# A transformer trunk on one core: two block pairs of the FFN's first product per layer as seven block products instead of eight

## The chip, the cores and the metric

The kernel runs on one core of one Trainium2 chip. The metric is the device time of one execution in microseconds (us); less is better.

## What is computed

Two layers of an encoder block over 256 tokens of width 1024, all in float32. The part that matters here, cut from the reference:

```python
h = h + rms_norm(mixed @ w_out, g_mix_post)                       # "wout"

gate, up = jnp.split(rms_norm(h, g_ffn_pre) @ w_ffn_in, 2, axis=-1)   # "ffnin": 1024 x 5632
h = h + rms_norm((jax.nn.silu(gate) * up) @ w_ffn_out, g_ffn_post)    # "ffnout": 2816 x 1024

e = p_i @ w_ple_proj                                              # "emb": 256 x 1024
h = h + rms_norm(jax.nn.sigmoid(h @ w_ple_gate) * e, g_ple_post)      # "ple"
```

Ahead of it in each layer stand one wide projection, gated linear attention and grouped-query attention, which the change does not touch.

## The kernel before

**Three matmuls for one product.** Each operand is kept as a high part rounded to the chip's float32r and a low part, the rest. `split` (L99) makes both: ScalarE copies (a CAST in the profile, L101), VectorE subtracts (L97). `mm3` (L87) then adds high x high, high x low and low x high into one PSUM bank. So a product of 128 tokens x 512 rows of weights x 512 columns is 4 x 3 = 12 matmuls of 128x512.

**The weight stream.** `plan` is the list of all weight units in the order of their use; a unit is 128 x 2048 (1 MB; 512 rows x 512 columns). `Stream` loads units on the SP queue into two `raw` buffers, splits each in two halves of 1024 into one of four pairs of buffers `wh` and `wl`, hands them out with `take` and gets them back with `done`. `ws = Stream(4)`: at most four units are split and not yet given back. `done` calls `fill`, which splits the next unit and starts the load behind it, so a split begins when TensorE has finished with the unit four before.

**ffnin.** The hidden width of 2816 is cut into 11 blocks of 256 (`NBLK`). A unit of a block holds 256 gate columns and 256 up columns for one half of the 1024 rows (`unit_gate_up`, L136), so a block is two units, and a unit is 24 matmuls: two token halves `hf` of 128 by 12. Blocks 0 and 1 go token half by token half with all four units held; blocks 2 to 10 go through `project` unit by unit. Then ScalarE takes silu of the gate half out of PSUM and VectorE multiplies by the up half ("gating"); some matmuls later TensorE transposes the result and `split` puts it into `hid`, the left operand of ffnout.

**Order of work around it.** The program is traced in one order, and a scheduler at compile time orders each engine's queue by it and by the times that it assumes. `tick()`, after every two rows of a unit's matmuls, counts down `Task`s, which put small work (transposes, attention steps) between the matmuls. `by_half` (L430) runs wout and ple with the first token half complete before the second, so that the norm of one half lies beside the matmuls of the other. Behind wout come the 24 matmuls of ple_proj (part "emb", L1015), and then ffnin (L1027), which needs the second half's norm after its first 36 matmuls. ffnout (L1075) and ple (L1109) follow. The input p is transposed ahead of wout.

**Buffers.** `big`: nine of 128 x 2048; `mid`: ten of 128 x 1024; `t512`: five; PSUM: eight banks (`acc`, `aux`).

Of the kernel before, what the change touches and what calls it, by code (L numbers as in the profile page):

```python
# [2 lines left out]

# [27 lines left out]
HIDDEN = 2816  # L31
NBLK = HIDDEN // 256
UNIT = 2112
RQ = ((0, 288), (288, 672), (672, 1056))
# [5 lines left out]
def trunk_kernel(ctx: ExitStack, tc: tile.TileContext, a: dict, out: bass.AP):  # L40
# [122 lines left out]
    for l in range(DEPTH):  # L163
        w = a["w_in"][l]
        plan += [unit_rows(w, n, C_RA, C_RA + 1056, 2 if l + n == 0 else 1) for n in range(4)]
        for c0 in (C_AK, C_GQ, C_GK, C_GV, C_GV + 512, C_GG, C_GG + 512, C_GA, C_GA + 512, C_GB, C_GB + 512):
            plan += [unit(w, kh, c0) for kh in range(2)]
        for j in range(2):
            for wo in (a["w_o_gla"][l], a["w_o_attn"][l]):
                plan += [unit(wo, kh, j * 512) for kh in range(2)]  # L170
        plan += [unit(a["w_out"][l], kh, j * 512) for kh in range(2) for j in range(2)]
        plan += [unit_rows(a["w_ple_proj"][l], 0)]
        plan += [unit_gate_up(a["w_ffn_in"][l], kh, b) for b in range(NBLK) for kh in range(2)]
        plan += [unit_rows(a["w_ffn_out"][l], n) for n in range(NBLK)]
        plan += [unit(a["w_ple_gate"][l], kh, j * 512) for kh in range(2) for j in range(2)]

    class Stream:


        def __init__(self, depth):  # L180
            self.depth, self.n, self.held, self.raws, self.ready, self.open = depth, 0, 0, [], [], False

        def load(self, between=lambda: None):

            if self.n == len(plan):
                return
            raw = rawp.tile([P, UNIT], F32, tag="raw", name=nm("raw"))
            moves = plan[self.n](raw)
            for dst, src in moves:
                if self.open:  # L190
                    nc.sync.dma_start(dst, src)
                else:
                    on("dma", nc.sync.dma_start, dst, src)
                between()
            self.raws.append((raw, sum(math.prod(dst.shape[1:]) for dst, _ in moves)))
            self.n += 1

        def pieces(self):

            raw, n = self.raws.pop(0)  # L200
# [4 lines left out]
            return [(wh[:, c], wl[:, c], raw[:, c]) for c in (slice(0, n // 2), slice(n // 2, n))]  # L205

        def fill(self):
            while self.open and self.held < self.depth and self.raws:
                for piece in self.pieces():
                    split(*piece)  # L210
                self.load()

# [4 lines left out]
        def done(self, n=1):  # L217
            self.held -= n
            self.fill()

# [37 lines left out]
    class Split:  # L258


        def __init__(self):
            self.h, self.l = (big(F32R).rearrange("p (k t) -> p k t", t=T) for _ in range(2))
            self.makers = {0: [], 1: []}

        def need(self, hf, k=None):
# [9 lines left out]
        def put(self, src, k, n, t0, tn):  # L275

            i = (slice(None), slice(k, k + n), slice(t0, t0 + tn))
            split(self.h[i], self.l[i], src.rearrange("p (k t) -> p k t", t=tn))

        def tok(self, k, hf):  # L280
            s = slice(hf * P, (hf + 1) * P)
            return self.h[:, k, s], self.l[:, k, s]

        def all(self, k):
            return self.h[:, k, :], self.l[:, k, :]

    def transpose_in(sp, src, k, n, hf):

        ps = aux()
        for i in range(n):  # L290
            nc.tensor.transpose(ps[:, i * P : (i + 1) * P], src[:, i * P : (i + 1) * P], ident)
        with tc.high_priority(AHEAD):
            sp.put(ps[:, : n * P], k, n, hf * P, P)

    last_pow = [None]
# [47 lines left out]

    def turn_in(sp, x, hf, wait):


        def turn():
            yield wait
            for j, y in enumerate(halves(x)):
                transpose_in(sp, y, 4 * j, 4, hf)  # L350

        sp.makers[hf].append(Task(turn(), part[0]))

    def pre_norm(g, hf, sp, wait=WAIT):

# [6 lines left out]

        turn_in(sp, xn, hf, wait)

# [27 lines left out]
    def wmode(os_, sp, k0, w, first, last):  # L392
# [9 lines left out]
        for f in range(4):  # L402
            o = os_[f // 2][:, (f % 2) * T : (f % 2 + 1) * T]
            s = slice(f * P, (f + 1) * P)
            for k in range(4):
# [3 lines left out]
                )  # L409
            tick()  # L410

    def project_t(sp):
# [113 lines left out]
    def turned(hf, k, n):  # L526

        ps = aux()
        for i in range(n):
            on("pe", nc.tensor.transpose, ps[:, i * P : (i + 1) * P], xn[hf][:, (k + i) * P : (k + i + 1) * P], ident)  # L530
        i = (slice(None), slice(k, k + n), slice(hf * P, (hf + 1) * P))
        split_here(uT.h[i], uT.l[i], ps[:, : n * P].rearrange("p (k t) -> p k t", t=P))

# [42 lines left out]
    for l in range(DEPTH):  # L576
# [413 lines left out]

        part[0] = f"{l}emb"
        e = big().rearrange("p (s c) -> p s c", s=2)
        pin = t512().rearrange("p (s c) -> p s c", c=256)
        nc.sync.dma_start(pin, a["p"][l, 0].rearrange("(s p) c -> p s c", p=P))
        pT = [t.rearrange("p (k t) -> p k t", t=T) for t in halves(mid(F32R))]
        ps = aux()
        for k in range(2):
            for hf in range(2):
                nc.tensor.transpose(
                    ps[:, k * T + hf * P : k * T + (hf + 1) * P], pin[:, hf, k * P : (k + 1) * P], ident  # L1000
                )
        split(pT[0], pT[1], ps.rearrange("p (k t) -> p k t", t=T))
# [4 lines left out]
        u2 = Split()  # L1007

        def after_out(hf, o):
            post_norm_add(o, gpost, hf)  # L1010
            pre_norm(gpre, hf, u2)

        by_half(mixT, after_out)

        part[0] = f"{l}emb"  # L1015
        wh, wl = (t[:, :2048].rearrange("p (k c) -> p k c", c=512) for t in ws.take())
        for hf in range(2):
            s = slice(hf * P, (hf + 1) * P)
            for j in range(2):
                o = acc()  # L1020
                for k in range(2):
                    mm3(o, (pT[0][:, k, s], pT[1][:, k, s]), (wh[:, 2 * k + j, :], wl[:, 2 * k + j, :]), k == 0, k == 1)
                nc.scalar.copy(e[:, hf, j * 512 : (j + 1) * 512], o)
        ws.done()


        part[0] = f"{l}ffnin"  # L1027
        hid = [Split() for _ in range(3)]
        us = [[ws.take() for _ in range(2)] for _ in range(2)]
        for hf in range(2):  # L1030
            for b in range(2):
                o = acc()
# [5 lines left out]
                nc.scalar.activation(sg[:, 0:256], o[:, 0:256], AF.Silu)  # L1038
                vmul(sg[:, 0:256], o[:, 256:512], sg[:, 0:256])


                def turn(sg=sg, b=b, hf=hf):
                    yield WAIT_FFN
                    transpose_in(hid[0], sg[:, 0:256], b * 2, 2, hf)

                hid[0].makers[hf].append(Task(turn(), part[0]))
        for b in range(2, NBLK):
            sg = t512()
            for hf, o in enumerate(project(u2)):
                c = slice(hf * 256, (hf + 1) * 256)  # L1050
                nc.scalar.activation(sg[:, c], o[:, 0:256], AF.Silu)
                vmul(sg[:, c], o[:, 256:512], sg[:, c])

            def turn(sg=sg, b=b):
                yield WAIT_FFN
                ps = aux()
                for k in range(2):
                    for hf in range(2):
                        nc.tensor.transpose(
                            ps[:, k * T + hf * P : k * T + (hf + 1) * P],  # L1060
                            sg[:, hf * 256 + k * P : hf * 256 + (k + 1) * P], ident,
                        )
                with tc.high_priority(AHEAD):
                    hid[b // 4].put(ps, 2 * b % 8, 2, 0, T)

            turned = Task(turn(), part[0], 2 * b % 8 // 4)
            for hf in range(2):
                hid[b // 4].makers[hf].append(turned)

        if l + 1 < DEPTH:  # L1070
            ropes = rope_tables(l + 1)
            wup_next = up_weights(l + 1)


# [5 lines left out]
        def out_step(n, hf, w):  # L1080
            wh, wl = (t[:, :2048].rearrange("p (k c) -> p k c", c=512) for t in w)
            for kk in range(2):
                k = 2 * n + kk
                hid[k // 8].need(hf, k % 8)
                for j in range(2):
                    mm3(
                        o[hf][j], hid[k // 8].tok(k % 8, hf), (wh[:, 2 * kk + j, :], wl[:, 2 * kk + j, :]),
                        k == 0, k == 2 * NBLK - 1,
# [10 lines left out]
        for hf in range(2):  # L1099
# [5 lines left out]

            turn_in(hT, h[:, hf, :], hf, WAIT_H)


# [77 lines left out]
```

## Time and profile before

| | |
|---|---|
| Time, median of 3 runs | 950.26 us (949.28 to 950.45) |
| The profiled execution | 950.44 us, span 948.7 us |
| TensorE clock granted | 0.998 of full speed |
| TensorE (PE) busy | 936.2 us, 99% of the span |
| VectorE (DVE) busy | 612.8 us, 65% |
| ScalarE (ACT) busy | 509.9 us, 54% |
| DMA | 169.25 MB, mean 178 GB/s |

In the profile a line starts with the line number in the kernel; names of buffers carry the layer and the part (`acc_0ffnin` is a PSUM bank of ffnin in layer 0). A group's row gives its count, its busy time and the mean duration in ns of one instruction; behind the last bar stands how long the engine was idle just before these, and what ended that. The chain of waits follows the work that ended last back from the end, and shows on which engine the time of the whole program lay.

### The profile page before, as it was taken

Reading aid. Unit: us, or ns where it says so; the run is one execution under the profiler, and the core shown is the slowest. Engines: PE = TensorE matmul, PEld = TensorE weight load, DVE = VectorE, ACT = ScalarE, POOL = GpSimd, SP = SyncE. Lnnn points to the kernel's source line nnn. Section 1 sums busy time; section 2 is a strip of 40 time slices with the busy share of each in tenths; the row PEclk is TensorE's granted clock in tenths of the full one; section 3 lists DMA queues with packets and bytes.
Section 4 is the critical chain, followed back from the end, with each engine's and each line's share of the span. In section 5 each row is a group of like instructions: output and inputs, shape, how many; then the busy total and the mean of one; then the engine's idle time right before and its main releaser. Section 6 shows DMA issues by size and latency. Waiting matters only on the chain.

```text
span 948.7 us, 12370 instructions
## 1 busy us (share of the span) xinstructions
PE 936.2 (99%) x4769; PEld 798.5 (84%) x4769; DVE 612.8 (65%) x838; ACT 509.9 (54%) x872; POOL 83.3 (9%) x152
## 2 busy tenths in 40 slices
PE   8999999999999999999999999999999999999996
PEld 7998888888888888888889988888888888888886
DVE  4798977456666555444779799663667665555364
ACT  4669776434465544443666686754436554443343
POOL 3400211000020000000133011200001000000010
PEclk9999999999999999999999999999999999999999
DMA  6463454655478655553545525355564666655531
GB/s 237 156 222 133 147 176 142 219 180 185 146 225 271 216 178 178 180 211 121 190 169 178 192 75 189 107 204 199 200 222 134 221 223 192 192 192 178 183 128 44
DMA packets 100760, 169.25 MB, mean 178 GB/s; under 512 B 3735, under 2 KB 51351, under 8 KB 100702
## 3 DMA queue, kind: packets, MB, share of 16 engines
q1 hardware_dynamic: 100702, 168.47, 52.7%
q8 instruction: 37, 0.61, 0.2%
q14 instruction: 21, 0.17, 0.0%
HBM read 167.41 MB, written 1.05 MB: 178 GB/s over the span
## 4 chain that ended last, share of the span: by engine, by line
PE 94%; DVE 2%; POOL 1%; ACT 1%; DMA 1%; issue 1%; SPq 0%; POOLq 0%; DVEq 0%; ACTq 0%
PE acc_0ffnin L85 13%; PE acc_1ffnin L85 13%; PE acc_0ffnout L85 6%; PE acc_1ffnout L85 6%; PE acc_0gate L85 5%; PE acc_1gate L85 5%; PE acc_1merge L85 5%; PE acc_0merge L85 5%; PE acc_1gqk L85 2%; PE acc_0rq L85 2%; PE acc_0gqk L85 2%; PE acc_1wout L85 2%; PE acc_0wout L85 2%; PE acc_1ple L85 2%; PE acc_1gg L85 2%; PE acc_0gg L85 2%
## 5 line engine op out<-in xcount | busy, mean ns | idle before, releaser
L85 PE MATMUL acc_0ffnin<-wh_0ffnin,big_0wout 128*128 128x512 f32 x288 | 91.3, 393 | 0.0
L85 PE MATMUL acc_1ffnin<-wh_1ffnin,big_1wout 128*128 128x512 f32 x288 | 91.3, 393 | 0.0
L97 DVE TENSOR_TENSOR wl_1ffnin<-raw_1ffnin,wh_1ffnin 128x1024 fp32r<-128x1024 f32 x40 | 47.9, 1221 | 48.4 <-ACT wh_1ffnin L101 48.4
L97 DVE TENSOR_TENSOR wl_0ffnin<-raw_0ffnin,wh_0ffnin 128x1024 fp32r<-128x1024 f32 x40 | 47.8, 1222 | 43.3 <-ACT wh_0ffnin L101 43.2
L101 ACT CAST wh_1ffnin<-raw_1ffnin 128x1024 fp32r<-128x1024 f32 x40 | 41.1, 1053 | 51.0 <-PE acc_1ffnin L85 38.2
L101 ACT CAST wh_0ffnin<-raw_0ffnin 128x1024 fp32r<-128x1024 f32 x40 | 40.8, 1052 | 44.7 <-PE acc_0ffnin L85 35.3
L85 PEld LDWEIGHTS acc_0ffnin<-wh_0ffnin,big_0wout 128*128 128x128 f32 x288 | 54.1, 188 | 11.0
L85 PEld LDWEIGHTS acc_1ffnin<-wh_1ffnin,big_1wout 128*128 128x128 f32 x288 | 54.1, 188 | 11.0
L85 PE MATMUL acc_1ffnin<-wl_1ffnin,big_1wout 128*128 128x512 f32 x144 | 56.1, 390 | 0.0
L85 PE MATMUL acc_0ffnin<-wl_0ffnin,big_0wout 128*128 128x512 f32 x144 | 56.1, 390 | 0.0
L85 PE MATMUL acc_0ffnout<-wh_0ffnout,big_0ffnin 128*128 128x512 f32 x112 | 34.9, 390 | 0.0
L85 PE MATMUL acc_1ffnout<-wh_1ffnout,big_1ffnin 128*128 128x512 f32 x112 | 34.9, 390 | 0.0
L97 DVE TENSOR_TENSOR wl_1ffnout<-raw_1ffnout,wh_1ffnout 128x1024 fp32r<-128x1024 f32 x18 | 21.3, 1222 | 18.4 <-ACT wh_1ffnout L101 18.4
L97 DVE TENSOR_TENSOR wl_0ffnout<-raw_0ffnout,wh_0ffnout 128x1024 fp32r<-128x1024 f32 x18 | 21.3, 1222 | 18.4 <-ACT wh_0ffnout L101 18.4
L85 PEld LDWEIGHTS acc_1ffnin<-wl_1ffnin,big_1wout 128*128 128x128 f32 x144 | 27.1, 188 | 5.3
L85 PEld LDWEIGHTS acc_0ffnin<-wl_0ffnin,big_0wout 128*128 128x128 f32 x144 | 27.1, 188 | 5.3
L101 ACT CAST wh_1ffnout<-raw_1ffnout 128x1024 fp32r<-128x1024 f32 x18 | 18.1, 1052 | 22.6 <-PE acc_1ffnout L85 22.6
L101 ACT CAST wh_0ffnout<-raw_0ffnout 128x1024 fp32r<-128x1024 f32 x18 | 18.2, 1053 | 22.5 <-PE acc_0ffnout L85 19.8
L97 DVE TENSOR_TENSOR wl_1gate<-raw_1gate,wh_1gate 128x1024 fp32r<-128x1024 f32 x14 | 16.5, 1222 | 17.8 <-ACT wh_1gate L101 17.8
L97 DVE TENSOR_TENSOR wl_0gate<-raw_0gate,wh_0gate 128x1024 fp32r<-128x1024 f32 x14 | 16.5, 1222 | 17.8 <-ACT wh_0gate L101 17.8
L85 PE MATMUL acc_0rq<-wh_start,big_start 128*128 128x384 f32 (+1 forms) x96 | 25.4, 349 | 0.9 <-ACT big_start L111 0.9
L85 PE MATMUL acc_0gate<-wh_0gate,big_start 128*128 128x512 f32 x80 | 24.8, 389 | 0.0
(587 smaller groups left out, 2672.7 us busy)
## 6 DMA issues: line engine op xcount, KB each, us to landing
raw_0ffnin<-in_w_ffn_in_dram SPq DMA_DIRECT2D x32, 512.0 KB, 4.2
raw_1ffnin<-in_w_ffn_in_dram SPq DMA_DIRECT2D x32, 512.0 KB, 3.9
raw_0ffnin<-in_w_ffn_out_dram SPq DMA_DIRECT2D x6, 1024.0 KB, 5.0
raw_1ffnin<-in_w_ffn_out_dram SPq DMA_DIRECT2D x6, 1024.0 KB, 4.9
raw_0ffnout<-in_w_ffn_out_dram SPq DMA_DIRECT2D x5, 1024.0 KB, 4.9
raw_1ffnout<-in_w_ffn_out_dram SPq DMA_DIRECT2D x5, 1024.0 KB, 4.9
raw_0rq<-in_w_in_dram SPq DMA_DIRECT2D x4, 1024.0 KB, 5.0
raw_0v<-in_w_in_dram SPq DMA_DIRECT2D x4, 1024.0 KB, 4.8
```

The costliest lines, as they stand in the source:

```text
L85: return nc.tensor.matmul(o, lhsT, rhs, start=start, stop=stop)
L97: nc.vector.tensor_tensor(out=out, in0=in0, in1=in1, op=ALU.subtract)
L101: nc.scalar.copy(hi, src)
```

## The change

Of ffnin's 11 blocks, 0 and 1 stay as they are, 4, 5, 8, 9 and 10 stay plain, and 2+3 and 6+7 become two pairs. A pair multiplies a 2 x 2 arrangement of left quarters (token half x row half: a11, a12, a21, a22) by a 2 x 2 arrangement of weight units (row half x gate or up: b11, b12, b21, b22, each 512 x 512), which takes 8 products of 12 matmuls. It now takes seven, with sums of the operands:

- P1 = a11 b11; P2 = (a12 - s2) b22 with s2 = a11 - a21 + a22; P3 = (a21 - a22)(b11 + b12); P4 = (a21 - a11)(b12 + b22); P5 = s2 (b11 + b12 + b22); P6 = a12 b21; P7 = a22 (b11 + b12 + b22 + b21).
- With v = P5 - P1 + P3, the results are c11 = P1 + P6 (added in P1's PSUM bank), c12 = v + P2, c22 = v + P4 and c21 = P3 + P7 - c22 (P7 is added in P3's bank); v and the other sums are made on VectorE.

The sums of the activations are made once per layer for both pairs (`sums`: four subtractions and four splits, from unsplit copies that `transpose_in` now also writes). The four sums of weights per pair are made in place in the raw tiles, step by step: b11 + b12 and b12 + b22 by transfers within SBUF that add into their destination, issued by GpSimd's queue; b11 + b12 + b22 and the one with b21 by VectorE. Each summed weight is split like a unit. The raw tiles of a pair are not the two `raw` buffers: b11 and b12 are loaded into a `wh` and a `wl` buffer lent for the pair (so that three pairs are left), b22 into a `big`, only b21 into a `raw`. `FFN_IN` lays the steps (1 to 7) between plain units (u).

`Split` now takes its tiles one for four rows, when they are first written, so `hid` is one `Split`. ple_proj's unit, its products and the transposes of p move from around wout to behind ffnout, ahead of ple.

```diff
+FFN_IN = "uu12u34u5u67uu12u34u5u67"
+WAIT_PAIR = 9
+PLAIN, PAIRS = (4, 5, 8, 9, 10), (2, 6)
 ...
+        plan += blocks[0] + blocks[1]
+        plains = [u for b in PLAIN for u in blocks[b]]
+        pairs = [[unit(w, kh, c + b * 256) for kh in range(2) for c in (0, HIDDEN)] for b in PAIRS]
+        for x in FFN_IN:
+            if x == "1":
+                pair = pairs.pop(0)
+            plan.append(plains.pop(0) if x == "u" else (pair, int(x)))
+        plan += [unit_rows(a["w_ffn_out"][l], n) for n in range(NBLK)]
         plan += [unit_rows(a["w_ple_proj"][l], 0)]
-        plan += [unit_gate_up(a["w_ffn_in"][l], kh, b) for b in range(NBLK) for kh in range(2)]
-        plan += [unit_rows(a["w_ffn_out"][l], n) for n in range(NBLK)]
 ...
+        def step(self, n, x, y, z, q):          # x, z, y, q: raw tiles of b11, b12, b22, b21
+            c = slice(0, 2048)
+            if n == 1:
+                self.made(x)
+                nc.gpsimd.dma_start(x.raw[:, c], z.raw[:, c], accum_op=ALU.add)
+            elif n == 2:
+                self.made(y)
+                nc.gpsimd.dma_start(z.raw[:, c], y.raw[:, c], accum_op=ALU.add)
+            elif n == 3:
+                self.made(x)
+                nc.vector.tensor_tensor(out=x.raw[:, c], in0=x.raw[:, c], in1=y.raw[:, c], op=ALU.add)
+            elif n == 4:
+                self.made(z)
+            elif n == 5:
+                self.made(x)
+                nc.vector.tensor_tensor(out=x.raw[:, c], in0=x.raw[:, c], in1=q.raw[:, c], op=ALU.add)
+            elif n == 6:
+                self.made(q)
+            else:
+                self.load()
+                self.made(x)
+                self.held -= 1
+                self.lend = True
 ...
+    def seven(sp, forms, gated):
+        made, task = forms
 ...
+        (p1, v), (p3, p7), (c12, c22) = (halves(mid()) for _ in range(3))
+        c11 = acc()
+        times(c11, quad(0, 0))                  # P1
+        nc.scalar.copy(p1, c11)
+        yield
+        task.need()
+        o = acc()
+        times(o, form(0))                       # P2
+        nc.scalar.copy(p3, o)
+        yield
+        p5 = acc()
+        times(p5, form(1))                      # P3
+        yield
+        o = acc()
+        times(o, form(2))                       # P4
+        nc.scalar.copy(p7, o)
+        yield
+        o = acc()
+        times(o, form(3))                       # P5
+        vsub(v, o, p1)
+        add(v, p5, v)
+        add(c12, v, p3)
+        add(c22, v, p7)
+        yield
+        times(c11, quad(0, 1), False)           # P6
+        gated(0, c11, c12)
+        yield
+        times(p5, quad(1, 1), False)            # P7
+        vsub(v, p5, c22)
+        gated(1, v, c22)
+        yield
```

(The comments are added here.)

More of the change, by code (lines that the diff above doesn't have):

```diff
@@ L2 @@
 from contextlib import ExitStack, nullcontext
+from itertools import chain
 import concourse.bass as bass
@@ L198, in pieces @@
-        def pieces(self):
-            raw, n = self.raws.pop(0)
+            self.depth, self.held, self.room, self.ready, self.open = depth, 0, 0, [], False
+            self.loads, self.jobs, self.lend = [], [], False
+            pairs = {}
+            for item in plan:
+                if callable(item):
+                    x = Load(item)
+                    self.loads.append(x)
+                    self.jobs.append(lambda x=x: self.plain(x))
+                else:
+                    units, n = item
+                    if n == 1:
+                        b11, b12, b21, b22 = units
+                        x, z = (Load(b, lambda tag=tag: self.lent(tag), tag == "wh") for b, tag in ((b11, "wh"), (b12, "wl")))
+                        y, q = Load(b22, big), Load(b21)
+                        pairs[id(units)] = x, y, z, q
+                        self.loads += [x, y, z]
+                    if n == 5:
+                        self.loads.append(q)
+                    self.jobs.append(lambda p=pairs[id(units)], n=n: self.step(n, *p))
@@ new lines, in lent, with start @@
+        def lent(self, tag):
+            if tag == "wh":
+                self.held += 1
+                self.lend = False
+            return wp.tile([P, UNIT], F32R, tag=tag, name=nm("lent")).bitcast(F32)
+        def load(self, between=lambda: None):
+            self.room += 1
+            self.start(between)
+        def start(self, between=lambda: None):
+            while self.loads and (self.lend or not self.loads[0].waits) and (self.loads[0].own or self.room):
+                x = self.loads.pop(0)
+                self.room -= not x.own
+                moves = x.start()
+                for dst, src in moves:
+                    if self.open:
+                        nc.sync.dma_start(dst, src)
+                    else:
+                        on("dma", nc.sync.dma_start, dst, src)
+                    between()
+                x.n = sum(math.prod(dst.shape[1:]) for dst, _ in moves)
@@ L218, in done @@
             self.held -= n
+            self.start()
             self.fill()
@@ L410, in wmode, with times, sums, make @@
             tick()
+    def times(o, act, first=True):
+        wh, wl = (t[:, :2048].rearrange("p (k c) -> p k c", c=512) for t in ws.take())
+        for k in range(4):
+            (ah, al), h, lo = act(k), wh[:, k, :], wl[:, k, :]
+            for n, (x, y) in enumerate(((ah, h), (ah, lo), (al, h))):
+                nc.tensor.matmul(
+                    o, x, y, start=first and k + n == 0, stop=k == 3 and n == 2, skip_group_check=not first
+                )
+            if k % 2:
+                tick()
+        ws.done()
+    def sums(x):
+        made = []
+        def make():
+            yield 1
+            (a11, a12), (a21, a22) = x
+            s2 = t512()
+            vsub(a22, a21, a22)
+            vsub(s2, a11, a22)
+            vsub(a12, a12, s2)
+            yield 1
+            vsub(a21, a21, a11)
+            for s in (a12, a22, a21, s2):
+                parts = halves(mid(F32R))
+                split(*parts, s)
+                made.append([p.rearrange("p (k t) -> p k t", t=P) for p in parts])
+                yield 1
+        return made, Task(make(), part[0])
+    def seven(sp, forms, gated):
+        made, task = forms
+        quad = lambda hf, j: lambda k: sp.tok(4 * j + k, hf)
+        form = lambda i: lambda k: [p[:, k, :] for p in made[i]]
+        def add(out, x, y):
+            nc.vector.tensor_tensor(out=out, in0=x, in1=y, op=ALU.add)
+        (p1, v), (p3, p7), (c12, c22) = (halves(mid()) for _ in range(3))
[29 more added lines that the diff above has]
+        yield
     def project_t(sp):
@@ L1007, in trunk_kernel, with turned, turn @@
         u2 = Split()
+        plain = [halves(mid()) for _ in range(2)]
         def after_out(hf, o):
             post_norm_add(o, gpost, hf)
-            pre_norm(gpre, hf, u2)
+            pre_norm(gpre, hf, u2, plain=plain[hf])
         by_half(mixT, after_out)
-        part[0] = f"{l}emb"
-        wh, wl = (t[:, :2048].rearrange("p (k c) -> p k c", c=512) for t in ws.take())
-        for hf in range(2):
[L1018 to L1030, printed above, removed]
+        part[0] = f"{l}ffnin"
+        hid = Split()
+        us = [[ws.take() for _ in range(2)] for _ in range(2)]
+        def turned(src, k, n, hf, wait=WAIT_FFN):
+            def turn():
+                yield wait
+                transpose_in(hid, src, k, n, hf)
+            hid.makers[hf].append(Task(turn(), part[0], k // 4))
+        for hf in range(2):
+            ws.lend = hf == 1
             for b in range(2):
@@ new lines, in pair, with gated @@
+        def pair(b):
+            def gated(hf, gate, up):
+                sg = t512()
+                nc.scalar.activation(sg, gate, AF.Silu)
+                vmul(sg, up, sg)
+                turned(sg, 2 * b, 4, hf, WAIT_PAIR)
+            return seven(u2, forms, gated)
+        steps, pairs, seven_ = chain.from_iterable(block(b) for b in PLAIN), list(PAIRS), None
+        for x in FFN_IN:
+            if x == "1":
+                seven_ = pair(pairs.pop(0))
+            next(steps if x == "u" else seven_)
@@ L1106, in trunk_kernel @@
             turn_in(hT, h[:, hf, :], hf, WAIT_H)
+        e = big().rearrange("p (s c) -> p s c", s=2)
+        embedded.need()
+        part[0] = f"{l}emb"
+        wh, wl = (t[:, :2048].rearrange("p (k c) -> p k c", c=512) for t in ws.take())
+        for hf in range(2):
+            s = slice(hf * P, (hf + 1) * P)
+            for j in range(2):
+                o = acc()
+                for k in range(2):
+                    mm3(o, (pT[0][:, k, s], pT[1][:, k, s]), (wh[:, 2 * k + j, :], wl[:, 2 * k + j, :]), k == 0, k == 1)
+                nc.scalar.copy(e[:, hf, j * 512 : (j + 1) * 512], o)
+        ws.done()
         part[0] = f"{l}ple"
```

156 lines of the change are left out of this document (90 added, 66 removed).

## The prediction

> **What bounds the kernel now.** I read the page's first part, then the chain that ended last, the groups of instructions by form, the chain again around the place that the change touches, and last the table of stretches and the DMA issues.
>
> ```profile
> PE 936.2 (99%) x4769; PEld 798.5 (84%) x4769; DVE 612.8 (65%) x838; ACT 509.9 (54%) x872; POOL 83.3 (9%) x152
> PE 94%; DVE 2%; POOL 1%; ACT 1%; DMA 1%; issue 1%; SPq 0%; POOLq 0%; DVEq 0%; ACTq 0%
> ```
>
> TensorE sets the end: 94% of the chain is its own matmuls, so a matmul taken away is worth its time if nothing else becomes late. Waiting is 12.5 us in all (948.7 less 936.2), and most of it lies at the start, between the layers and at the end.
>
> ```profile
> 258.21 2.88 PE acc_0wout L85 x24
> 261.09 5.47 PE acc_0emb L85 x24
> 266.55 8.17 PE acc_0ffnin L85 x36
> 274.72 0.87 PE aux_0wout L291 x8
> 275.59 2.75 PE acc_0ffnin L85 x12
> ...
> 306.97 10.93 PE acc_0ffnin L85 x48
> 317.90 0.44 PE aux_0ffnin L1059 x4
> ```
>
> This is the chain of layer 0 from wout's end. Columns: start, length, work. A plain block of ffnin is 48 matmuls in 10.93 us and its transposes in 0.44. One 512-wide matmul costs the chain 10.93/48 = 0.228 us (its own 0.393 us in the groups overlaps the next). So 24 matmuls (one weight unit) take 5.46 us and 12 take 2.73.
>
> ```profile
> L97 DVE TENSOR_TENSOR wl_0ffnin<-raw_0ffnin,wh_0ffnin 128x1024 fp32r<-128x1024 f32 x40 | 47.8, 1222 | 43.3 <-ACT wh_0ffnin L101 43.2
> L101 ACT CAST wh_0ffnin<-raw_0ffnin 128x1024 fp32r<-128x1024 f32 x40 | 40.8, 1052 | 44.7 <-PE acc_0ffnin L85 35.3 <-DMA raw_0ffnin<-in_w_ffn_in_dram 9.4
> L94 DVE TENSOR_TENSOR t_0ffnin<-acc_0ffnin,t_0ffnin 128x256 f32<-128x256 f32 x22 | 9.2, 420 | 2.9 <-ACT t_0ffnin L1038 2.8
> L97 DVE TENSOR_TENSOR big_0ffnin<-aux_0ffnin,big_0ffnin 128x512 fp32r<-128x512 f32 x9 | 6.2, 685 | 1.6 <-ACT big_0ffnin L101 1.6
> 290.00:386.00 96.00, 96.00 (x440) 79.44 (x439) 54.53 (x63) 46.28 (x63) 0.00 (x0) 1.00 0.64 207
> ```
>
> VectorE's price list: 0.42 us at 256 wide, 0.69 at 512, 1.22 at 1024. The last line is a stretch of plain blocks (columns: stretch, length, PE, PEld, DVE, ACT, POOL, clock, DMA share, GB/s): VectorE is busy 54.53 of 96 us, ScalarE 46.28, the DMA engines 0.64 of the time for 207 GB/s.
>
> **What the change takes away.** Two blocks cost 4 units x 24 = 96 matmuls; seven products of 12 are 84. Per pair 12 x 0.228 = 2.73 us, four pairs in two layers: 10.92 us. Transposes stay as many, ple_proj's 24 matmuls only move.
>
> **What it adds on VectorE.** A pair was 8 half splits (9.78), 4 gatings (1.68) and 2 transposed pieces (1.37): 12.8 us. It becomes 14 half splits (17.11), two weight sums of 2048 elements (0.53 more per 512 in the rows, so 1.22 + 2 x 0.53 = 2.29 each, 4.58), five operations on products (3.44), two gatings of 512 (1.38) and two pieces (1.37): 27.9. With the five plain units of a section (2.5 blocks: 12.2 + 2.1 + 1.7 = 16.0) it is 43.9 us of work beside 5 x 5.46 + 7 x 2.73 + 1.95 of transposes = 48.4 us of TensorE: 91%. The first section of a layer also has the four activation sums and their splits, 8 x 0.69 = 5.5 us: 49.4, over 100%. ScalarE comes to 24 casts (25.2) and some 7 us: two thirds. So VectorE has next to no spare time here, and only the run-ahead covers it: three weights are held ahead, as one of the four pairs of buffers is lent. A split may begin when TensorE has finished the product three before, thus 5.5 to 10.9 us before it is needed, against some 3.5 us from its start to its end.
>
> I walk the first section through, t = 0 where block 0's second unit is done. Unstalled, TensorE starts u 5.5, u 10.9, P1 16.4, P2 19.1, u 21.8, P3 27.3, P4 30.0, u 32.8, P5 38.2, u 41.0, P6 46.4, P7 49.1. VectorE, in order of arrival, is about 4.4 us late at 10.9 (15.3 us of work by then) and ends P2's split at 19.5, P3's at 25.9, the sum behind it at 28.2, P4's at 30.7, u's at 33.1, P5's at 35.6: each one's first half is just in time. At P7 the queue bites: P7 adds into the bank that the operation v = P5 + v still reads, and that operation stands behind P7's split and the next unit's. In this order it is done at 50.6, 1.5 us late. If products go first it costs nothing; I take 1.0 per layer for this and for P4 below. In the second section the 4.5 us of spare time clear the backlog, and I find no wait.
>
> **What it adds on the DMA engines and POOL.** Per pair two adding transfers of 1 MB, the second overwriting what the first reads, so one behind the other; P3's split waits for the first and P4's for the second, and behind these stand, on ScalarE and VectorE both, the next unit's split and the gatings. No row shows such a transfer. Below, it costs no less than a plain load of 1 MB, 4.9 to 5.0 us.
>
> ```profile
> raw_0ffnin<-in_w_ffn_out_dram SPq DMA_DIRECT2D x6, 1024.0 KB, 5.0
> ```
>
> 207 GB/s at a share of 0.64 is 323 at full use, so 1 MB is 3.3 us of engine time and 1.6 us fixed. An addition reads two operands: 6.5 + 1.6 = 8.1 us, which I take, as few loads are due in that stretch. If loads slow it in proportion to their 0.64 share, it is 6.5 x 1.64 + 1.6 = 12.3, my upper end. A first pair's transfers start between 9 us (splits first) and 13.4 (arrival order), say 11.2; P4 needs its first half at 30.0, 2.3 us (a cast and a subtraction) after the second: d may be (30.0 - 2.3 - 11.2)/2 = 8.25 us. A second pair's weights are loaded when a buffer falls free at 46.4, the last is there at 46.4 + 4.9 + 3.3 = 54.6, P4 is at 76.4: d may be 9.75. At 8.1 both just fit. POOL has nothing else in these stretches that anyone waits for.
>
> The Trainium skill (DMA: Bandwidth & Descriptors, Anatomy of one DMA) fits a gpsimd transfer as 2.0 us and the bytes at 436 GB/s, an estimate of 4.4 us for 1 MB and, for a read of both operands, 6.8; by it no pair would wait at P4, and the sum would lose up to 2 us more. No row here shows it.
>
> **What moves.** ple_proj's products stood right behind wout's and covered the norm of the second token half. Without them, ffnin starts at 261.09, and the transposes, 8.17 us later, at 269.26; the normalized halves were ready at 269.5 and 270.2:
>
> ```profile
> 268.77 1.41 DVE L339 SCALAR_TENSOR_TENSOR mid_0wout<-h,rstd_0wout,mid_0wout 128x512 f32<-128x512 f32 x2 [1.36 <-POOL rstd_0wout L335]
> ```
>
> That is 0.5 us of wait, and the splits behind them, which had 2.7 us and needed them, share ScalarE with two new copies: 0.7 per layer taken; bounds 0 (the norm runs faster, as four copies of ple_proj's products leave ScalarE) and 2.5 (ScalarE's table load and both copies ahead of it). Between ffnout and ple the moved products only lengthen a gap in which nothing waited; nothing gained, nothing lost. SP's loads keep their number; weights of a pair go to their own tiles.
>
> **Sum.** 950.44 (the profiled execution; span 948.7 and 1.7 around it) - 10.92 + 2 x 0.7 + 2 x 1.0 = 942.9; that execution lies 0.18 over the median of 950.26, so 942.7.
>
> **Rivals.** *The adding transfers set the pace* (slower). Past 8.25 and 9.75 us each extra microsecond counts twice, so a layer loses 4d - 36 and both 8d - 72. Against the 9.5 us that are left after the norm's wait it decides at d = 10.2. At 11 us the time is 956.8, at 12.3 it is 950.3 - 9.5 + 26.4 = 967.2. For it: loads fill 0.64 of the engines' time, and the chain of two has no slack at my own 8.1. Against: in that stretch only one or two loads are due. The Trainium skill (DMA: Bandwidth & Descriptors, Queues, rings and completion order) says that each DMA engine takes turns between its queues packet by packet, so a load delays an addition as much as it has packets; by that rule d is nearer 12.3 when loads are always pending, and this rival follows. The page before has only one busy queue, so its trace cannot show it. Chance 0.28.
>
> *VectorE becomes the bound.* Before, it idled 43.3 us ahead of the splits for ScalarE's casts. If in every section a third of its 12 splits' casts (4 x 1.05) were not covered, first sections would take 49.4 + 4.2 = 53.6 of 48.4 and second ones 48.1: some 5 us per layer, 950.3 - 9.5 + 10 = 951. Against: the next cast runs while VectorE subtracts. Chance 0.11.
>
> *Nothing waits:* 950.26 - 10.92 = 939.3. It needs VectorE to take products first and transfers under 8 us. Chance 0.13.
>
> **How the numbers follow.** My forecast 942.7 has 0.48. The range, 939 to 960, reaches into the first rival up to d = 11.4 (8 x 11.4 - 72 = 19.2, so 960) and leaves out some 0.15 above. About 0.2% is what a measurement of this kernel tells from no change. Faster: 0.48 + 0.13, and 0.02 of the first rival where its transfers are only just too long, 0.63; same: most of the VectorE rival, 0.09; slower: the other 0.26 of the first and 0.02 of VectorE's, 0.28.
>
> **What would show it.** In the profile after: 48 matmuls fewer, TensorE busy about 925 us; adding transfers of 7 to 9 us to landing; VectorE near 90% in the pair stretches and some 684 us in all (612.8 + 4 x 15.1 + 2 x 5.5); TensorE's waits at P4 and P7 of the first pair and at the transposes behind wout, together 1 to 2 us per layer. Wrong: ScalarE's casts of summed weights waiting for a DMA of over 10 us with TensorE idle behind them, or TensorE waiting for lower weight halves all through a section.

## The result and the profile after

| | before | after |
|---|---|---|
| Time, median | 950.36 us (949.28 to 950.56) | 959.02 us (958.73 to 959.99) |
| Profiled execution, span | 950.44, 948.7 us | 959.99, 958.3 us |
| TensorE clock granted | 0.998 | 0.993 |
| TensorE busy | 936.2 us | 931.9 us |
| VectorE busy | 612.8 us | 678.9 us |

The changed kernel is slower: ratio 1.0095, 95% interval 1.0078 to 1.0113, or 8.7 us. I forecast 942.7. The time lies in the range given, on the other side of no change. That it lies inside is luck: by the formula of the rival that reaches so far, the adding transfers would have to take 11.3 us each, and they took 8.64 in the mean.

Of the page of the changed kernel, its first line, the queue of the adding transfers and the chain's shares:

```profile
PE 931.9 (97%) x4721; PEld 791.1 (83%) x4721; DVE 678.9 (71%) x898; ACT 544.8 (57%) x916; POOL 94.4 (10%) x160
q0 software_dynamic: 1152, 8.39, 4.5%
PE 11%; DMA 5%; DVE 2%; issue 1%; ACT 1%; POOLq 0%; POOL 0%; DVEq 0%; ACTq 0%; SPq 0%
```

The 48 matmuls are gone (4769 to 4721), yet TensorE is busy only 4.3 us less, and 26.4 us of the span (958.3 - 931.9) are now without a matmul, where it was 12.5. The 8.39 MB of this queue are the eight adding transfers. The chain's shares add up to a fifth of the span only: followed back from the end it breaks off in layer 1, at the first adding transfer there, so the shares stand for that part alone. What TensorE waits for in ffnin (columns: what waits, releaser, us in total, times, longest):

```profile
PE acc_1ffnin L527 <- ACT wh_1ffnin L106: 4.4, 1, 4.4
PE aux_0ffnin L1238 <- DVE t_0ffnin L99: 2.8, 3, 1.1
PE acc_1ffnin L527 <- DVE wl_1ffnin L102: 2.2, 2, 1.5
PE aux_1ffnin L1238 <- DVE t_1ffnin L99: 2.2, 2, 1.2
PE acc_0ffnin L527 <- DVE wl_0ffnin L102: 0.9, 1, 0.9
PE acc_0ffnin L90 <- DVE wl_0wout L102: 0.5, 2, 0.3
```

L527 is a product of a pair, L1238 the transposes of the gated pieces, L99 a gating. The forecast had 0.7 us per layer for the splits of the last row, 1.0 per layer for the products of pairs, and nothing for the transposes. The chain shows the largest one, in layer 1's first pair:

```profile
758.58 0.97 DMA lent_1ffnin<-lent_1ffnin
759.55 8.23 issue
767.79 12.44 DMA lent_1ffnin<-big_1ffnin
...
780.41 0.11 ACT wh_1ffnin L106
...
782.58 1.23 DVE wl_1ffnin L102
...
783.85 4.28 PE acc_1ffnin L527 x11
```

The second adding transfer (b12 + b22) takes 12.44 us; P4's cast follows it at once, then its subtraction, and TensorE with them. The last row holds a second loss: 11 matmuls in 4.28 us, where 11 x 0.228 are 2.51. The table of stretches gives the reason (columns: stretch, length, PE, PEld, DVE, ACT, POOL, clock, DMA share, GB/s):

```profile
775.00:780.00 5.00, 2.14 (x10) 1.44 (x8) 0.00 (x0) 0.00 (x0) 0.00 (x0) 1.00 0.93 228
780.00:785.00 5.00, 1.95 (x4) 1.25 (x5) 3.03 (x4) 4.59 (x6) 0.00 (x0) 0.52 0.01 5
785.00:790.00 5.00, 5.00 (x19) 3.98 (x18) 4.97 (x5) 2.74 (x4) 0.00 (x0) 0.80 0.30 82
```

After the wait the granted clock is 0.52, then 0.80: matmuls stand 0.427 us apart, not 0.228. The first row shows a third thing: for 5 us neither VectorE nor ScalarE does anything, though a transposed piece and the next unit's splits are queued behind P4's cast. Layer 0 shows how, in ScalarE's and VectorE's timelines (start, length, work, idle before and its releaser):

```profile
308.00 1.05 ACT L106 CAST wh_0ffnin<-lent_0ffnin 128x1024 fp32r<-128x1024 f32 x1 [6.46 <-DMA lent_0ffnin<-big_0ffnin]
```

```profile
309.56 0.69 DVE L102 TENSOR_TENSOR big_0ffnin<-aux_0ffnin,big_0ffnin 128x512 fp32r<-128x512 f32 x1 [4.73 <-ACT big_0ffnin L106]
```

P4's cast stands at the head of ScalarE's queue for 6.46 us. A transposed piece's copy stands behind it, though its data is there, and VectorE waits 4.73 us for that copy. P4 itself is only 0.9 us late here. In layer 0's second pair P4 isn't late at all, and there the order of ScalarE's queue shows the rest:

```profile
358.27 2.00 ACT L106 CAST wh_0ffnin<-lent_0ffnin 128x1024 fp32r<-128x1024 f32 x2 [5.85 <-DMA lent_0ffnin<-big_0ffnin]
...
360.65 0.39 ACT L1230 ACTIVATE t_0ffnin<-acc_0ffnin 128x256 f32<-128x256 f32 x1
...
362.81 0.39 ACT L1230 ACTIVATE t_0ffnin<-acc_0ffnin 128x256 f32<-128x256 f32 x1
```

The two silus (L1230) of the plain unit ahead stand behind P4's cast, which waits 5.85 us; their gatings follow on VectorE with splits between them, and a transpose comes 1.1 us late. The groups carry the sum (behind the last bar, idle time and what ended most of it):

```profile
L106 ACT CAST wh_1ffnin<-lent_1ffnin 128x1024 fp32r<-128x1024 f32 x20 | 20.2, 1050 | 21.6 <-DMA lent_1ffnin<-big_1ffnin 17.5
L106 ACT CAST wh_0ffnin<-lent_0ffnin 128x1024 fp32r<-128x1024 f32 x20 | 20.2, 1050 | 13.9 <-DMA lent_0ffnin<-big_0ffnin 12.3
```

### The profile page after: what moved, and what is told of

Read it like the earlier page. It is cut to its first block, busy times and chain, and to the rows that moved or that the text cites. A ratio compares the mean times of both kernels' runs of the same rounds, so it can differ in the third digit from the quotient of the medians.

```text
span 958.3 us, 12373 instructions
## 1 busy us (share of the span) xinstructions
PE 931.9 (97%) x4721; PEld 791.1 (83%) x4721; DVE 678.9 (71%) x898; ACT 544.8 (57%) x916; POOL 94.4 (10%) x160
## 3 DMA queue, kind: packets, MB, share of 16 engines
q0 software_dynamic: 1152, 8.39, 4.5%
## 5 line engine op out<-in xcount | busy, mean ns | idle before, releaser
L90 PE MATMUL acc_0ffnin<-wh_0ffnin,big_0wout 128*128 128x512 f32 x160 | 51.8, 394 | 0.0
L90 PE MATMUL acc_1ffnin<-wh_1ffnin,big_1wout 128*128 128x512 f32 x160 | 51.7, 393 | 0.0
L102 DVE TENSOR_TENSOR wl_1ffnin<-raw_1ffnin,wh_1ffnin 128x1024 fp32r<-128x1024 f32 x28 | 32.9, 1220 | 8.0 <-ACT wh_1ffnin L106 7.9
L90 PEld LDWEIGHTS acc_0ffnin<-wh_0ffnin,big_0wout 128*128 128x128 f32 x160 | 30.0, 188 | 6.1
L90 PEld LDWEIGHTS acc_1ffnin<-wh_1ffnin,big_1wout 128*128 128x128 f32 x160 | 30.0, 188 | 6.1
L106 ACT CAST wh_1ffnin<-lent_1ffnin 128x1024 fp32r<-128x1024 f32 x20 | 20.2, 1050 | 21.6 <-DMA lent_1ffnin<-big_1ffnin 17.5
L90 PE MATMUL acc_0ffnin<-wl_0ffnin,big_0wout 128*128 128x512 f32 x80 | 31.2, 390 | 0.0
L90 PE MATMUL acc_1ffnin<-wl_1ffnin,big_1wout 128*128 128x512 f32 x80 | 31.2, 390 | 0.0
L106 ACT CAST wh_1ffnout<-raw_1ffnout 128x1024 fp32r<-128x1024 f32 x18 | 18.1, 1052 | 21.3 <-PE acc_1ffnout L90 18.7
L102 DVE TENSOR_TENSOR wl_0ffnout<-raw_0ffnout,wh_0ffnout 128x1024 fp32r<-128x1024 f32 x18 | 21.3, 1221 | 11.4 <-ACT wh_0ffnout L106 11.3
L102 DVE TENSOR_TENSOR wl_1ffnin<-lent_1ffnin,wh_1ffnin 128x1024 fp32r<-128x1024 f32 x20 | 23.5, 1218 | 7.3 <-ACT wh_1ffnin L106 7.3
L106 ACT CAST wh_0ffnin<-lent_0ffnin 128x1024 fp32r<-128x1024 f32 x20 | 20.2, 1050 | 13.9 <-DMA lent_0ffnin<-big_0ffnin 12.3
```

What stands on the lines that cost most here:

```text
L90: return nc.tensor.matmul(o, lhsT, rhs, start=start, stop=stop)
L102: nc.vector.tensor_tensor(out=out, in0=in0, in1=in1, op=ALU.subtract)
L106: nc.scalar.copy(hi, src)
```

## The experiments

The theory: the products save what was forecast; the loss comes from instructions that wait for a transfer at the head of an in-order queue, from work queued behind them that VectorE can't make up, and from TensorE's clock after its waits. Rivals: the moved ple_proj; VectorE's load as such; the transfers' traffic.

**The move alone.** No pairs and no sums of activations; ple_proj stays behind ffnout.

```diff
-FFN_IN = "uu12u34u5u67uu12u34u5u67"
-PLAIN, PAIRS = (4, 5, 8, 9, 10), (2, 6)
+FFN_IN = "u" * 18
+PLAIN, PAIRS = (2, 3, 4, 5, 6, 7, 8, 9, 10), ()
 ...
-        plain = [halves(mid()) for _ in range(2)]
+        plain = [None, None]
 ...
-                if (hf, b) == (1, 0):
-                    forms = sums(plain)
```

> No pairs: all blocks plain, only the move of ple_proj's products and the new layout of the split tiles are left of the change. Theory A (the second adding transfer is late at P4, and the wait halves TensorE's clock) and theory B (ScalarE and VectorE run their queues full, so that transposes wait for gatings): 951 to 952, a wait of 0.5 to 1 us per layer at the transposes behind wout. Theory C (the move costs more than the waits that were read there): 954 or more.

Measured: 952.27 us (950.47 to 953.75), ratio 1.0024 [1.0012, 1.0036]: 2 us. The profiled execution took 953.49 us; its span is 3.1 us longer than before's, and 1.3 of these lie with the clock: layer 1's first projection takes 28.28 us in this trace and 26.99 before, with the same wait of 1.4 us some 9 us into it, after which the clock falls here and not there. The move isn't the loss.

**No adding transfers.** The two transfers of each pair are left out, and with them the sums b11 + b12 and b12 + b22.

```diff
-                nc.gpsimd.dma_start(x.raw[:, c], z.raw[:, c], accum_op=ALU.add)
-                nc.gpsimd.dma_start(z.raw[:, c], y.raw[:, c], accum_op=ALU.add)
```

> The two adding transfers of each pair are left out (so the weight sums lack b12 and b22 in P3, P4, P5 and P7); everything else as after. Theory A: the waits at P4 (about 10 us with the slow clock) go, 947 to 949. Theory B: only a few of them go, because casts and gatings are late all the same, 954 to 957.

Measured: 940.32 us (938.66 to 941.18), ratio 0.9897 [0.9877, 0.9916], below what either theory expected. TensorE is busy 925.9 us of a span of 938.8, and between 280 and 379 us it has no idle time, with VectorE at 88%:

```profile
280.00:379.00 99.00, 99.00 (x451) 81.86 (x450) 87.34 (x93) 64.58 (x84) 3.76 (x2) 1.00 0.55 183
```

So the transfers cost 18.7 us (959.02 - 940.32), and VectorE's load alone costs next to nothing. From ffnin's first matmul to ffnout's first it is 120.69 and 120.31 us in the two layers here, and 125.82 and 132.10 in the changed kernel: 16.9 us of the loss lie inside ffnin.

**P4 later.** One plain unit is laid between P3 and P4, taken from between P5 and P6.

```diff
-FFN_IN = "uu12u34u5u67uu12u34u5u67"
+FFN_IN = "uu12u3u4u567uu12u3u4u567"
```

> The order uu12u3u4u567: one more plain unit (5.46 us) between P2 and P4, and 5, 6, 7 back to back. Theory A: the second adding transfer has 5.5 us more, the wait at P4 is gone in three pairs and short in the fourth, 950 to 953. Theory B: three products in a row with four 512-wide operations load VectorE more, and the gain at P4 is lost at P6, P7 and the transposes, 957 to 961.

Measured: 949.65 us (947.25 to 953.68), ratio 0.9999 [0.9982, 1.0016]. In the trace (of an execution of 953.07 us) TensorE's waits at P4 are gone, and in the median half of the loss; waits at the transposes stay:

```profile
PE aux_1ffnin L1238 <- DVE t_1ffnin L99: 2.9, 2, 2.3
...
PE aux_0ffnin L1238 <- DVE t_0ffnin L99: 1.9, 1, 1.9
```

P4 has its weights in time, and still the gatings are late.

**Transposes later.** The gated pieces are transposed after 8 ticks instead of 4.

```diff
-WAIT, WAIT_FIRST, WAIT_NEXT, WAIT_H, WAIT_FFN, WAIT_MIX = 6, 4, 9, 5, 4, 3
+WAIT, WAIT_FIRST, WAIT_NEXT, WAIT_H, WAIT_FFN, WAIT_MIX = 6, 4, 9, 5, 8, 3
```

> The transposes of gated blocks come 8 ticks behind the block instead of 4 (some 5.5 us later). Theory B: the 5.2 us of waits at these transposes are gone, 953 to 955. Theory A: they only show a queue that is late for P4's sake, so the time moves to the next wait, 957 to 959.

Measured: 960.94 us (955.78 to 963.15), ratio 1.0108 [1.008, 1.0136]; nothing gained, and more than either theory expected. In the trace (of the fastest execution, 955.78 us) the waits at the transposes are gone, and P4 of a second pair waits in each layer instead, 1.8 us for its cast and 1.8 for its subtraction:

```profile
PE acc_0ffnin L527 <- DVE wl_0ffnin L102: 1.8, 1, 1.8
PE acc_1ffnin L527 <- DVE wl_1ffnin L102: 1.8, 1, 1.8
PE acc_0ffnin L527 <- ACT wh_0ffnin L106: 1.8, 1, 1.8
PE acc_1ffnin L527 <- ACT wh_1ffnin L106: 1.7, 1, 1.7
```

**All four sums on VectorE**, nothing left out.

```diff
-                nc.gpsimd.dma_start(x.raw[:, c], z.raw[:, c], accum_op=ALU.add)
+                nc.vector.tensor_tensor(out=x.raw[:, c], in0=x.raw[:, c], in1=z.raw[:, c], op=ALU.add)
 ...
-                nc.gpsimd.dma_start(z.raw[:, c], y.raw[:, c], accum_op=ALU.add)
+                nc.vector.tensor_tensor(out=z.raw[:, c], in0=z.raw[:, c], in1=y.raw[:, c], op=ALU.add)
```

> All four weight sums of a pair on VectorE, no adding transfers. VectorE then has 48.5 us of work beside 48.4 of TensorE in a section. Theory A (what is lost is the wait for the results of the transfers): the 2.29 us of a sum is cheaper than the wait, 942 to 946. Theory B (VectorE's queue is the limit as soon as it is full): waits of 2 to 4 us in each section, 950 to 955.

Measured: 942.17 us (941.85 to 943.65), ratio 0.9927 [0.9911, 0.9942]: faster than both kernels, with VectorE busier than in the changed one (695.7 us). A busy VectorE that waits for no transfer is fast enough.

**The two sums on GpSimd**, in the same two lines (`nc.gpsimd.tensor_tensor`).

> The two transferred sums by GpSimd's own addition instead. From the rope rows of before (128x256 in 0.74 us, 128x64 in 0.29 us) 128x2048 is estimated at 4.9 us, against 7 to 12 for a transfer, and no traffic. If GpSimd and VectorE do not hinder each other: 940 to 943. If they do (a rope row of 128x256 took 3.07 us in the profile after, where VectorE was busy): additions of 10 us and more and longer VectorE instructions, 950 to 965.

Measured: 969.76 us (968.62 to 970.1), ratio 1.0212 [1.0197, 1.0228], above what I expected even for engines that hinder each other. The sums take 4.6 to 5.4 us each, shorter than a transfer, but VectorE's subtractions beside them grow, in this group from 1.22 to 4.41 us in the mean:

```profile
L102 DVE TENSOR_TENSOR wl_1ffnin<-big_1ffnin,wh_1ffnin 128x1024 fp32r<-128x1024 f32 x4 | 17.6, 4407 | 0.2 <-ACT wh_1ffnin L106 0.2
```

The Trainium skill (SBUF — State Buffer, Who interferes with whom) says that a VectorE instruction with two SBUF inputs contends with a GpSimd instruction that reads SBUF; the trace agrees. TensorE then waits 6.1 and 6.3 us at the transposes, as it does behind a late VectorE in the changed kernel.

**The first sum on VectorE, the second still a transfer.**

```diff
-                nc.gpsimd.dma_start(x.raw[:, c], z.raw[:, c], accum_op=ALU.add)
+                nc.vector.tensor_tensor(out=x.raw[:, c], in0=x.raw[:, c], in1=z.raw[:, c], op=ALU.add)
```

> Only b11 + b12 goes to VectorE; b12 + b22 stays an adding transfer, which now has no transfer before it and over 15 us until P4. Theory A: P4's wait is gone, VectorE has 46.2 us of 48.4: 941 to 944. Theory A2 (the transfers do harm by slowing the loads, not by their results): half of the 18.7 us that leaving both out brought, 948 to 951.

Measured: 942.04 us (940.94 to 943.06), ratio 0.9922 [0.9906, 0.9938]: four transfers of 7.0 to 8.1 us remain and cost next to nothing, because each has landed before its cast comes to the head of the queue. The group of the casts names no DMA any more, and TensorE is at 99% again:

```profile
L106 ACT CAST wh_1ffnin<-lent_1ffnin 128x1024 fp32r<-128x1024 f32 x20 | 20.2, 1050 | 5.2 <-ACT wh_1ffnin L106 1.5 <-ACT t_1ffnin L1230 1.4 <-PE acc_1ffnin L90 0.8
```

```profile
PE 926.3 (99%) x4721; PEld 788.5 (84%) x4721; DVE 688.3 (73%) x902; ACT 547.3 (58%) x916; POOL 91.4 (10%) x156
```

So a transfer as such was no fault.

**Both transfers, read by nobody.** They add into a spare buffer; left out are the two sums that the products need. In a first pair the first one starts 4.1 to 4.5 us earlier than in the changed kernel, counted from ffnin's first matmul, as it doesn't wait for b11's split; the second starts 0.7 and 1.8 us earlier.

```diff
-                nc.gpsimd.dma_start(x.raw[:, c], z.raw[:, c], accum_op=ALU.add)
+                x.spare = big()
+                nc.gpsimd.memset(x.spare, 0.0)
+                nc.gpsimd.dma_start(x.spare, z.raw[:, c], accum_op=ALU.add)
 ...
-                nc.gpsimd.dma_start(z.raw[:, c], y.raw[:, c], accum_op=ALU.add)
+                nc.gpsimd.dma_start(x.spare, y.raw[:, c], accum_op=ALU.add)
```

> Both adding transfers run as in after, at the same places and one behind the other, but into a spare tile that nothing reads, so P3, P4, P5 and P7 take weights without these sums, as in the run without adding transfers. Theory A: nobody waits, 940 to 943. Theory A2: the traffic is the same as after, so are most of the losses, 950 to 958.

Measured: 940.09 us (939.66 to 941.21), ratio 0.9904 [0.9889, 0.9919]: as without transfers, though they take 7.3 to 11.2 us. Here their traffic harms nobody.

**The first sum a transfer, the second on VectorE**: the reverse of the version that was faster.

```diff
-                nc.gpsimd.dma_start(z.raw[:, c], y.raw[:, c], accum_op=ALU.add)
+                nc.vector.tensor_tensor(out=z.raw[:, c], in0=z.raw[:, c], in1=y.raw[:, c], op=ALU.add)
```

> The other half of the run with the first sum on VectorE: b11 + b12 stays an adding transfer, b12 + b22 goes to VectorE, behind it. Theory A with the chain of two as its cause: one transfer of 7 to 9 us from t = 13 is there by 22, long before P3 at 27.3, and VectorE's sum of 2.29 us follows: 941 to 944, like its counterpart. If any transfer that starts behind P1's split is too late: 948 or more.

Measured: 956.06 us (953.18 to 956.72), ratio 1.005 [1.0033, 1.0066]; I had expected a gain. The one transfer left is short (7.0 to 8.9 us), but VectorE's sum overwrites what it reads, so now VectorE's own queue stands. Its timeline, and TensorE's largest wait:

```profile
768.52 2.29 DVE L285 TENSOR_TENSOR lent_1ffnin<-lent_1ffnin,big_1ffnin 128x2048 f32<-128x2048 f32 x1 [5.54 <-DMA lent_1ffnin<-lent_1ffnin]
```

```profile
PE aux_1ffnin L1238 <- DVE t_1ffnin L99: 4.8, 2, 3.8
```

A gating and the next unit's split stand behind this sum. No row has a product of a pair waiting for its weights: the loss comes through the queue, not through late sums.

**b22's load behind b11's and b12's**, on the thought that the 12.44 us came from loads just ahead of the transfer.

```diff
-                        self.loads += [x, y, z]
+                        self.loads += [x, z, y]        # and y's load issued after z's
```

> As after, but b22's load is queued behind those of b11 and b12, so that the second pair's does not run just ahead of the first pair's second transfer. If the 12.4 us of that transfer in layer 1 came from the 2.1 MB of loads queued before it, it takes 7 to 9 us, and the long wait with the slow clock in layer 1 (8.8 us) shrinks to the 1 us of layer 0: 950 to 953. If its length has another cause: 957 to 960.

Measured: 961.17 us (960.12 to 963.33), ratio 1.0117 [1.0095, 1.0138]: missed. The longest transfer fell to 10.3 us, but the others now took 8.1 to 9.9, and TensorE still waited 8.5 us in all for weights of pairs and 5.0 us at the transposes.

**Late load and P4 later together.**

> Late load of b22 and the order uu12u3u4u567 together, both adding transfers kept. Theory A (the results come too late, nothing else): both transfers now fit, 941 to 945. If the two remedies do not add up, 948 to 950.

Measured: 947.97 us (946.44 to 949.71), ratio 0.9981 [0.9969, 0.9993]: far better than the late load alone, while against P4 later alone (949.65) the intervals overlap. The transfers took 7.9 to 10.9 us; waits of 2.4 and 1.1 us at the transposes stay.

**A wait that nobody needs.** To the unread transfers (sums left out as there) a one-column copy on VectorE is added that waits for the second transfer, and the first transfer again waits for b11's split.

```diff
+                nc.vector.tensor_copy(x.spare[:, 0:1], self.ready[-1][1].bitcast(F32)[:, 0:1])
 ...
             elif n == 4:
                 self.made(z)
+                nc.vector.tensor_copy(small(1, "ss1"), x.spare[:, 0:1])
```

> Left out, as in e8: the two sums of weights that a pair needs; both adding transfers add into a spare buffer that no product reads. Added to e8: the first transfer waits again for b11's split (one column copied by VectorE into the spare buffer), and behind the step that makes P4's weights VectorE copies one column of the spare buffer into a tile that nobody reads, so that VectorE's queue waits for the second transfer while TensorE needs nothing of it. In the first pair of a layer this copy stands right behind P3's split, with the sum behind it, the transposed piece and P4's split queued behind; in the second pair just ahead of P3's split. My theory (the loss comes from the head of the in-order queue that stands waiting, and TensorE waits for what is queued behind it, then at half its clock): most of the loss comes back, 950 to 960 us, with TensorE's waits at the lower halves (L102) and at the transposes of the gated pieces. Rival A (TensorE loses only by the lateness of the summed weights themselves, or by the engines' bytes): 939 to 941 us as e8. Rival B (VectorE catches up from such a wait at once, and only ScalarE's cast at the head counts): 941 to 945 us.

Measured: 967.86 us (965.8 to 972.09), ratio 1.0202 [1.0175, 1.023]: all of the loss is back, and 8 us above the top of what I expected, with no product reading what a transfer made. VectorE's timeline in layer 1's first pair, and TensorE's waits:

```profile
782.95 0.15 DVE L294 COPY ss_1ffnin<-big_1ffnin 128x1 f32<-128x1 f32 x1 [10.70 <-DMA big_1ffnin<-big_1ffnin]
```

```profile
PE acc_1ffnin L531 <- DVE wl_1ffnin L102: 10.2, 3, 6.7
PE acc_0ffnin L531 <- DVE wl_0ffnin L102: 3.9, 3, 1.6
PE aux_0ffnin L1242 <- DVE t_0ffnin L99: 3.0, 3, 1.1
PE aux_1ffnin L1242 <- DVE t_1ffnin L99: 2.0, 2, 1.2
```

An instruction of 0.15 us holds VectorE 10.70 us; its four waits come to 30.6 us, and the time grows by 27.8 (967.86 - 940.09). Here a wait at VectorE's head lies at a worse place than in the changed kernel, where most waits stood on ScalarE, so the two losses are not to be set equal; the mechanism is the same. The first transfer also starts as late as in the changed kernel again; what that alone would cost beside the unread transfers was not run.

## Why the prediction was wrong, step by step

- **What the change takes away: right.** 48 matmuls, and without the transfers 940.32. Before's median of its batch less 10.92 is 939.4; what is left for everything else is 0.9 us.
- **What it adds on VectorE: right in the prices and in the verdict.** A sum of 2048 took 2.29 us as worked out; 678.9 us in all against 684. The rival that VectorE becomes the bound fell twice (no transfers; all sums on VectorE at 942.17). Of the 1.0 us per layer for P7 and P4, P7's part didn't come: no row shows it.
- **What moves: about right.** 1.4 us for both layers was taken. The move alone measured 2.0; in its trace ffnin is 1.1 and 0.7 us longer in the two layers than before, and 1.3 us come from the clock in another stage, which no step of mine had.
- **The size of d: right as a mean, wrong as one number.** The eight transfers took 7.18, 8.56, 7.72, 8.38, 8.62, 12.44, 6.94 and 9.30 us from issue to landing, 8.64 in the mean, against 8.1. The 12.44 is about the upper end I had kept (12.3), met once, with two loads just ahead of it; the sign of being wrong that I had named, a cast that waits for a transfer of over 10 us with TensorE idle behind it, came there.
- **The step that failed: the limits on d, and the price behind them** ("At 8.1 both just fit"). They asked when P4 needs its weights, and took lateness there as the whole price. But the instruction that waits holds its queue from the moment it comes to the head, well before P4, and what is queued behind it has earlier dates: a piece's copy, gatings, the next splits. I had named these ("behind these stand, on ScalarE and VectorE both, the next unit's split and the gatings") and put no price on them. Layer 0's second pair, with a transpose late and P4 in time, is the plain case. My rival's formula has the same fault. With the measured lengths only layer 1's first pair passes its limit, by 4.6 us (8.62 + 12.44 - 2 x 8.25), and TensorE's wait for P4's cast there was 4.4: as the price of P4's lateness it holds, but 18.7 us were lost.
- **The clock had no place in the sum.** After 4.4 us without work the matmuls ran at half rate; at P4 of layer 1's first pair the matmuls stood 8.2 us further apart in all than at full pace, of which the wait for the cast was 4.4, that for the subtraction 1.5, and the clock's share the other 2.3.

How the loss divides, by the starts of the stages in the two traces, whose spans differ by 19.5 us (958.3 - 938.8): 5.1 and 11.8 in the two layers' ffnin, 1.3 in layer 1's first projection with its clock, and 1.2 before layer 0's ffnin and behind layer 1's. Of the 11.8, 8.8 are TensorE's waits in the rows above (4.4 + 2.2 + 2.2) and 2.3 the clock at P4; of the 5.1, 3.7 are waits (2.8 + 0.9). What is shown: the transfers are needed for the loss, their traffic and VectorE's load are not, and a wait at a queue's head brings a loss as large without any sum being read. Not separated by a run: what the clock costs in ffnin with the waits left as they are; the 2.3 us are read from one trace.

## What to carry to other kernels

A transfer whose result an in-order engine waits for must have landed before the waiting instruction comes to its queue's head, not before its result is needed; price everything queued behind it, above all on an engine that is busy for nine tenths of the time. A single transfer that nothing stood waiting for was free here. Two in a chain were not, and neither was a single one with a VectorE sum waiting for it (956.06 us). Four sums of 2.29 us on the busy engine in place of the chains' first transfers were cheaper. The version with the first sum on VectorE ran in 942.04 us, the one with all of them in 942.17; both beat both kernels, and no interval here tells them apart.

## What the runs showed of the hardware

- **The granted clock fell after some waits of TensorE and not after others.** 4.4 us of wait were followed by a granted clock of 0.52 over 5 us. A wait of 1.4 us in layer 1's first projection, with one of 0.3 us behind it, was followed by 0.76 over 4 us in the changed kernel (first row) and by 1.00 in the kernel before (second row). The Trainium skill (TensorE: Matmul & The Clock Gate, What's actually happening) has a free-running window of some 3.4 us, so that the place in the window decides; that fits both, though a wait of 1.4 us, with one of 0.3 us behind it, already suffices here.

```profile
488.00:492.00 4.00, 3.33 (x16) 2.91 (x17) 4.00 (x6) 2.67 (x4) 0.00 (x0) 0.76 0.00 0
488.00:492.00 4.00, 3.59 (x22) 2.87 (x23) 4.00 (x5) 2.34 (x3) 0.00 (x0) 1.00 0.03 4
```

- **An adding transfer within SBUF of 1 MB took 6.94 us at the least.** In the 12.44 us case its first packet moved 5.2 us after the issue, against 1.4 to 1.7 in the other seven, with two loads issued 1.2 and 0.8 us before it; in the last experiment, with the same two loads ahead, it was 5.0 us. The Trainium skill (DMA: Bandwidth & Descriptors, Queues, rings and completion order) has each engine take turns between its queues packet by packet; in these two cases only packets of the loads' queue moved for those first 5 us, and what held the transfer back is not shown.
- **GpSimd's additions stretched VectorE's two-input work** from 1.22 to 4.4 us in the mean of four; one in layer 0's first pair took 5.61.
